# One PSUM tile per prompt head, and an attention end written out for every engine

## The chip, the core and the metric

The kernel runs on one NeuronCore of one Trainium2 chip. The metric is device time in microseconds (us) of one execution. The engines are PE (TensorE matmuls; its weight loads are listed apart as PEld), DVE (VectorE), ACT (ScalarE), POOL (GpSimd) and SP (SyncE, which here only issues loads).

## What is computed

One inference step of a two-layer trunk. Each layer takes 256 prompt tokens and 8 samples of 8 new tokens (320 columns in all) through one input projection, three token mixers, and a gated sum:

```
x += W_out( sum_b sigmoid(gate_b(xn)) * P_b( branch_b(xn) * silu(z_b) ) ), xn = RMSNorm(x)
  A: multi-scale causal pooling mixer
  B: multi-head latent attention (low-rank q and kv, rotary key, absorbed form)
  C: gated DeltaNet
```

Branch B (MLA) has 8 heads. The prompt attends to itself; each sample attends to 2048 cached tokens, gathered by a page table, and to its own 8.

## The kernel before

Values are fp32. A large product is done as three fp32r matmuls per 128 rows of contraction (`mm3`, lines 220 to 222): high weight by high input, high weight by low input, low weight by high input. So each weight block is split first: `split_w` writes the high part `wh` on ACT (line 196) and the low part `wl` on DVE (line 197). An input is split in the same way by `split_x` or `split_y` (`yH` on ACT, line 202; `yL` on DVE, line 203).

Each layer has a projection part, ordered by a scheduler, and then an attention part whose order on PE, DVE, ACT and POOL is the order of the code (`tc.manual_schedule`). The attention part has two stages.

- **Head stage.** The loop `for h in range(11)` goes through the 8 prompt heads as a pipeline. For head h: scores `hsc` on PE (`head_scores`, lines 1278 and 1279), two maxima on DVE (1283, 1284), two exponentials on ACT (1289, 1290, output `pS`). Two steps later come the reciprocal on DVE (1294), the scaling on POOL (1295, 1296), three transposes `pT` on PE (1301) and their copy `pPT` on ACT (1303). One step after that comes `po`, the product with the values (1310), and its use on DVE (1312). Two gate products (`gate`, 24 matmuls each) lie between the heads, one half at a time, and DVE also turns the first sample's keys (`flip`, 1164 and 1167). The scores of all heads are slices of one tile of four PSUM banks. After the heads come the first sample's scores `sc` (1177).
- **Sample stage.** The loop `for bb in range(NB)` goes through the 8 samples. For each one: the exponential, one or two gate products, the transposes `PT` and `PTn`, the 34 matmuls `pv` (1248, 1252), and in the next step the product `olat` (1260), which reorders the result.

Then comes the end of the attention: 24 branch products `br` (3 branches by 8 blocks `m`; 12 matmuls each) with `oml` (32 small matmuls that end the MLA branch) among the first ones, and then the output projection. In `branch(n, m)`, n = 0 is the pooling branch with input y0 = `zs[0:4]`, n = 1 the DeltaNet branch with `zs[8:12]`, and n = 2 the MLA branch with `zs[4:8]`, which is ready only after `oml`. These products stand outside the hand-ordered part, so the scheduler places them; it also puts some of their weight splits back into the sample loop. In layer 1 one gate product is left over after the loop (`if order: gate("A")`), and the scheduler mixes its matmuls with the first branch products. All products rotate through PSUM tiles with tag `A`: four banks during the attention, and after it a newly opened pool (four banks in layer 0, six in layer 1).

Of the kernel before, what the change touches and what calls it, by code (L numbers as in the profile page):

```python
# [116 lines left out]
def trunk(tc, I, O, layers=2):  # L117
# [7 lines left out]
    @contextmanager  # L125
    def phase(name, psum, side="left"):

        with tc.tile_pool(name=name, bufs=1, side=side, reuse_waits="tile") as sb, tc.tile_pool(name=name + "_ps", bufs=1, space=PSUM, reuse_waits="tile") as pp:
            old = dict(banks), dict(wcfg)
            banks.clear()  # L130
            banks.update(pool=pp, n=psum)
            wcfg.clear()
            yield sb
            banks.clear()
            wcfg.clear()
            banks.update(old[0])
            wcfg.update(old[1])

    def ps(tag, name):
        return banks["pool"].tile([128, 512], F32, tag=tag, name=name, bufs=banks["n"][tag])  # L140

# [268 lines left out]
    for l in range(layers):  # L410
# [719 lines left out]
        olat = p2.tile([128, 2, 8, 64], F32, tag="qlat", name="olat", bufs=1)  # L1130
        p2b, pa = enter(f"pa_{l}", dict(A=4, S=1), "right")
        pdc, phc, pbc = ExitStack(), ExitStack(), ExitStack()
        pd = pdc.enter_context(tc.tile_pool(name=f"pd_{l}", bufs=1, reuse_waits="tile"))
# [35 lines left out]
        def scores(keys, q4):  # L1169

            KT, krT = keys
            sc = banks["pool"].tile([128, 4, 512], F32, tag="S", name="sc", bufs=1)
# [143 lines left out]

        def split_y(pool, y0):
            yb[y0] = (pool.tile([128, 4, T], F32R, name=f"yH{y0}"), pool.tile([128, 4, T], F32R, name=f"yL{y0}"))
            for i in range(4):
                split_x(yb[y0][0][:, i, :], yb[y0][1][:, i, :], zs[y0 + i])  # L1320

        def branch(n, m, tag):
            if (n, m) in spilled:
                t = per.tile([128, T], F32, tag="gt", name="gt", bufs=NG)
                nc.gpsimd.dma_start(t, spilled[n, m])
            else:
                if (n, m) not in early:
                    gate("pj")
                t = early[n, m]
            _, wname, y0 = branches[n]  # L1330
            w = split_w(load_w(I[wname][l][:, m * 128 : m * 128 + 128], 4, 128)[:, :4, :], 4)
            b = ps(tag, "br")
            mm3(b[:, :T], w, yb[y0], 4)
            if n == 0:
                accs[m] = p3a.tile([128, T], F32, tag="acc", name="acc", bufs=4)
                stt(accs[m], t, 1.0, b[:, :T], add, mult)
            else:
                stt(t, t, 1.0, b[:, :T], add, mult)
                nc.gpsimd.tensor_tensor(accs[m], accs[m], t, add)


        with tc.manual_schedule(engines={mybir.EngineType.PE, mybir.EngineType.DVE, mybir.EngineType.Activation, mybir.EngineType.Pool}):
# [9 lines left out]
            nm, w = gate_w()  # L1352
            hsc = banks["pool"].tile([128, 4, 512], F32, tag="S", name="hsc", bufs=1)

# [7 lines left out]
            keys = key_tiles()  # L1362
            flips = {3: 0, 4: 1, 5: 2, 6: 3, 7: 4}
            hs, hp = {}, {}
            b = sc = None
            for h in range(11):
                if h < 8:
                    head_scores(h, hsc[:, h % 4])
                    st2 = head_max(hsc[:, h % 4])
                    hs[h] = head_soften(hsc[:, h % 4], st2), st2  # L1370
                if h < 2:
                    values(h)
                if h == 4:
                    gather(1)
                if h in flips:
                    flip(0, keys, flips[h])
# [19 lines left out]
                if h == 9:  # L1396
                    sc = scores(keys, q4)
            phc.close()
            pb = pbc.enter_context(tc.tile_pool(name=f"pb_{l}", bufs=1, side="right", reuse_waits="tile"))
# [38 lines left out]
            wuv = load_wuv(pb.tile([128, 1024], F32, tag="S", name="wuv", bufs=2))  # L1438
            pdc.close()
            p3e = ExitStack()  # L1440
            p3a = p3e.enter_context(tc.tile_pool(name=f"p3a_{l}", bufs=1, reuse_waits="tile"))
            yb = {}
            split_y(p3a, 0)
        branch(0, 0, "A")
        combined(NB - 1, combine(o))
        if order:
            gate("A")
        branch(0, 1, "A")
        b = ps("A", "oml")
        for p in range(4):  # L1450
            for e in range(2):
                h = 2 * p + e
                for cc in range(2):
                    nc.tensor.matmul(b[64 * e : 64 * e + 64, p * 64 : p * 64 + 64], wuv[:, cc, h * 64 : h * 64 + 64], olat[:, cc, h, :], start=cc == 0, stop=cc == 1)
        for p in range(4):
            stt(zs[4 + p][:, TP:], b[:, p * 64 : p * 64 + 64], 0.5, zs[4 + p][:, TP:], mult, mult)
        pbc.close()
        p2b.close()
        p2c.close()
        pec.close()  # L1460


        last = l == layers - 1
        p3c, p3 = enter(f"p3_{l}", dict(pj=2, A=6) if last else dict(pj=4, A=4))
        wcfg.update(pool=p3, n=2)
        split_y(p3, 8)
        split_y(p3, 4)
        mg = (p3.tile([128, 8, T], F32R, name="mgH"), p3.tile([128, 8, T], F32R, name="mgL"))
        xT = p3.tile([128, 8, T], F32, name="xT")
        nc.gpsimd.dma_start(xT, xs[l])  # L1470
        for mp in range(4):
            for n in range(3):
                for m in (2 * mp, 2 * mp + 1):
                    if n or m > 1:
                        branch(n, m, "A")
# [3 lines left out]
        if last:  # L1479

            y6 = [ps("A", "yo") for _ in range(6)]
            t0s = (0, 128, 192)
# [26 lines left out]
        else:  # L1509
# [9 lines left out]
            nc.sync.dma_start(O["y_sample"].rearrange("b s d -> (b s) d"), yo[64:, 2, :])  # L1519
        p3c.close()  # L1520
        p3e.close()
    ctx.close()
# [27 lines left out]
```

## Time and profile before

| | |
|---|---|
| device time, median of 3 runs | 1057.81 us (1056.7 to 1057.89) |
| profiled execution | 1062.18 us |
| its span | 1060.1 us |
| PE busy in the span | 995.1 us (94%) |
| DVE, ACT, POOL busy | 708.6 (67%), 465.0 (44%), 329.5 us (31%) |
| mean granted PE clock | 0.968 of full |

The span is the time from the first to the last instruction in the trace. Times in the trace are in us from the start of the span; layer 0's attention part lies at about 284 to 470 us and layer 1's at about 802 to 990 us.

### The profile page before, as it was taken

Reading aid. Unit: us, or ns where it says so; the run is one execution under the profiler, and the core shown is the slowest. Engines: PE = TensorE matmul, PEld = TensorE weight load, DVE = VectorE, ACT = ScalarE, POOL = GpSimd, SP = SyncE. Lnnn points to the kernel's source line nnn. Section 1 sums busy time; section 2 is a strip of 40 time slices with the busy share of each in tenths; the row PEclk is TensorE's granted clock in tenths of the full one; section 3 lists DMA queues with packets and bytes.
Section 4 is the critical chain, followed back from the end, with each engine's and each line's share of the span. In section 5 each row is a group of like instructions: output and inputs, shape, how many; then the busy total and the mean of one; then the engine's idle time right before and its main releaser. Section 6 shows DMA issues by size and latency. Waiting matters only on the chain. (4 is left out here: it accounts for less than half of the span.)

```text
span 1060.1 us, 24775 instructions
## 1 busy us (share of the span) xinstructions
PE 995.1 (94%) x10211; PEld 869.1 (82%) x10211; DVE 708.6 (67%) x1353; ACT 465.0 (44%) x838; POOL 329.5 (31%) x467
## 2 busy tenths in 40 slices
PE   8989899999989999989989978989999999999996
PEld 6877798887878887779978867979887778777996
DVE  3899984558556666568659878645674657674872
ACT  5554353454543333344546624326445333334453
POOL 3566321215240101035345542212234211000631
PEclk7999999999989999999999979999999999999998
DMA  8533333633746776258563322345264477742861
GB/s 232 154 81 99 100 84 91 182 96 113 211 131 191 245 232 228 79 166 249 141 200 82 99 80 72 99 133 133 81 161 156 150 255 220 248 156 86 262 177 50
DMA packets 202698, 159.22 MB, mean 150 GB/s; under 512 B 27704, under 2 KB 191826, under 8 KB 200010
## 3 DMA queue, kind: packets, MB, share of 16 engines
q1 hardware_dynamic: 176364, 98.47, 34.3%
q0 software_dynamic: 7424, 48.75, 12.8%
q10 hardware_dynamic: 18798, 10.44, 3.4%
q8 instruction: 80, 1.31, 0.5%
q14 instruction: 32, 0.26, 0.1%
HBM read 144.17 MB, written 13.68 MB: 149 GB/s over the span
## 5 line engine op out<-in xcount | busy, mean ns | idle before, releaser
L197 DVE TENSOR_TENSOR wl<-wraw,wh 128x1024 fp32r<-128x1024 f32 (+2 forms) x169 | 195.2, 1164 | 80.3 <-ACT wh L196 79.6
L196 ACT ACTIVATE wh<-wraw 128x1024 fp32r<-128x1024 f32 (+1 forms) x180 | 166.2, 935 | 165.2 <-PE pj L221 77.8
L220 PE MATMUL pj<-xnH,wh 128*128 128x320 f32 (+1 forms) x528 | 175.4, 332 | 16.9 <-DVE V L497 6.1
L222 PE MATMUL pj<-xnH,wl 128*128 128x320 f32 (+1 forms) x528 | 172.4, 327 | 7.4 <-DVE wl L197 7.1
L221 PE MATMUL pj<-xnL,wh 128*128 128x320 f32 (+1 forms) x528 | 170.7, 323 | 0.0
L220 PE MATMUL gate<-xnH,wh 128*128 128x320 f32 x384 | 125.1, 326 | 1.7 <-DVE V L497 1.5
L220 PEld LDWEIGHTS pj<-xnH,wh 128*128 128x128 f32 (+1 forms) x528 | 103.8, 197 | 23.3 <-ACT wh L196 8.3
L222 PE MATMUL gate<-xnH,wl 128*128 128x320 f32 x384 | 120.5, 314 | 1.6 <-DVE wl L197 1.3
L221 PE MATMUL gate<-xnL,wh 128*128 128x320 f32 x384 | 119.7, 312 | 0.0
L222 PEld LDWEIGHTS pj<-xnH,wl 128*128 128x128 f32 (+1 forms) x528 | 103.5, 196 | 11.8 <-DVE wl L197 9.1
L221 PEld LDWEIGHTS pj<-xnL,wh 128*128 128x128 f32 (+1 forms) x528 | 103.7, 196 | 5.2 <-issue 3.8
L220 PEld LDWEIGHTS gate<-xnH,wh 128*128 128x128 f32 x384 | 72.9, 190 | 9.3 <-issue 5.7
L1167 DVE STREAM_TRANSPOSE KT<-kv 128x1024 f32<-128x1024 f32 x64 | 78.6, 1228 | 0.4
L222 PEld LDWEIGHTS gate<-xnH,wl 128*128 128x128 f32 x384 | 72.7, 189 | 3.0 <-DVE wl L197 1.8
L221 PEld LDWEIGHTS gate<-xnL,wh 128*128 128x128 f32 x384 | 73.0, 190 | 1.0 <-issue 0.8
L220 PE MATMUL br<-yH,wh 128*128 128x320 f32 x192 | 59.7, 314 | 5.2 <-ACT wh L196 3.3
L1248 PE MATMUL pv<-kv,PT 128*64 128x256 f32 x512 | 58.8, 382 | 2.3 <-ACT PT L1226 2.3
L1177 PE MATMUL sc<-KT,q 32*64 32x256 f32 x2048 | 59.3, 377 | 0.0
L221 PE MATMUL br<-yL,wh 128*128 128x320 f32 x192 | 59.1, 309 | 0.0
L222 PE MATMUL br<-yH,wl 128*128 128x320 f32 x192 | 58.4, 309 | 0.0
L505 DVE SCALAR_TENSOR_TENSOR cy<-V,prm,cy 128x344 f32<-128x344 f32 x72 | 56.4, 803 | 0.5
L1177 PEld LDWEIGHTS sc<-KT,q 32*64 32x64 f32 x2048 | 45.8, 131 | 12.0 <-issue 5.7
(410 smaller groups left out, 2046.8 us busy)
## 6 DMA issues: line engine op xcount, KB each, us to landing
wraw<-in_w_in SPq DMA_DIRECT2D x114, 512.0 KB
wraw<-in_w_out SPq DMA_DIRECT2D x16, 512.0 KB
q<-q4d SPq DMA_DIRECT2D x64, 72.0 KB
gate<-gt ACTq DMA_DIRECT2D x28, 160.0 KB
gt<-gate POOLq DMA_DIRECT2D x28, 160.0 KB, 3.7
wraw<-in_w_br_pool SPq DMA_DIRECT2D x16, 256.0 KB
wraw<-in_w_br_dn SPq DMA_DIRECT2D x16, 256.0 KB
wraw<-in_w_br_mla SPq DMA_DIRECT2D x16, 256.0 KB
```

The costliest lines, as they stand in the source:

```text
L196: act(h, raw, AF.Copy)
L197: (nc.gpsimd.tensor_tensor if spare or turn[0] in K["lo"] else tt)(lo, raw, h.bitcast(F32), sub)
L220: nc.tensor.matmul(out, wh[:, k, :], xh[:, first + k, :], start=k == 0, stop=False)
L221: nc.tensor.matmul(out, wh[:, k, :], xl[:, first + k, :], start=False, stop=False)
L222: nc.tensor.matmul(out, wl[:, k, :], xh[:, first + k, :], start=False, stop=k == nk - 1)
L505: stt(y, V[:, j : j + 344], wj(j), y, mult, add)
L1167: nc.vector.transpose(v[:, a], kv[:, a * 1024 : a * 1024 + 1024].rearrange("p (i k c) -> p i k c", i=4, k=8))
L1177: nc.tensor.matmul(sc[64 * hf : 64 * hf + 64, g, :256], q4[r, k, :], krT[r, keys_] if k == 8 else KT[r, k, keys_], start=k == 0, stop=k == 8,)
L1248: nc.tensor.matmul(pv[64 * hf : 64 * hf + 64, :256], PT[:, n * 128 + 64 * hf : n * 128 + 64 * hf + 64], kv[:, r : r + 256], start=n == 0, ...
```

## The change

There are four parts.

1. **A PSUM tile per head.** `hsc` becomes a tile of one bank for each head, out of four (tag `H`).
2. **Two moves in the head loop.** The second gate's split (`gate_w`) goes from the end of step 4 to step 5, behind head 5's exponentials. Three flips go one step later.
3. **The end is written out.** `branch` is cut into `branch_w` (load and split of the weight), `branch_mm` (the product) and `branch_out` (its use). Seven branch products, (0,0), (0,1), (1,0), (1,1), (0,2), (2,0) and (2,1), now stand in the hand-ordered part, in a fixed order on all engines. In the last sample's step, y0 is split ahead of the exponential, product (0,0) stands between `PTn` and `pv`, and y8 is split ahead of `pv`. The leftover gate of layer 1 stands behind product (0,1).
4. **Banks kept open.** The four `A` banks get a pool of their own, which stays open to the end of the layer. The pool after the attention has four other banks (layer 0) or two and two (layer 1), so that layer 1's branch products rotate through four banks and no longer six.

```diff
+        apc = ExitStack()
+        banks["A"] = apc.enter_context(tc.tile_pool(name=f"aps_{l}", bufs=1, space=PSUM, reuse_waits="tile"))
...
-            flips = {3: 0, 4: 1, 5: 2, 6: 3, 7: 4}
+            flips = {3: 0, 4: 1, 6: 2, 7: 3, 8: 4}
...
-                    head_scores(h, hsc[:, h % 4])
-                    st2 = head_max(hsc[:, h % 4])
-                    hs[h] = head_soften(hsc[:, h % 4], st2), st2
+                    hsc = hp_.tile([128, 512], F32, tag="H", name="hsc", bufs=4)
+                    head_scores(h, hsc)
+                    st2 = head_max(hsc)
+                    hs[h] = head_soften(hsc, st2), st2
...
+                if h == 5:
+                    nm, w = gate_w()
...
-                if h == 4:
-                    nm, w = gate_w()
...
+                if not more:
+
+                    pdc.close()
+                    p3a = p3e.enter_context(tc.tile_pool(name=f"p3a_{l}", bufs=1, reuse_waits="tile"))
+                    split_hi(p3a, 0)
                 S = soften(bb, sc, mx)
...
+                else:
+                    split_lo(0)
+                    w00 = branch_w(0, 0)
...
+                if not more:
+                    b00 = branch_mm(0, w00, "A")
                 weigh(bb, mx)
+                if not more:
+                    w01 = branch_w(0, 1)
+                    split_y(p3a, 8)
                 o = attend(bb, PT, PTn, mx)
...
+            branch_out(0, 0, b00)
+            b01 = branch_mm(0, w01, "A")
+            if order:
+                gate("A")
+            w10 = branch_w(1, 0)
+            combined(NB - 1, combine(o))
+            b10 = branch_mm(1, w10, "A")
+            branch_out(0, 1, b01)
+            w11 = branch_w(1, 1)
+            b = ps("A", "oml")
...
+            b11 = branch_mm(1, w11, "A")
+            spc.close()
+            pbc.close()
+            mc.close()
+            p2c.close()
+            pec.close()
...
+            p3c, p3 = enter(f"p3_{l}", dict(pj=2, Y=2) if last else dict(pj=4))
+            wcfg.update(pool=p3, n=2)
+            w20 = branch_w(2, 0)
+            split_y(p3, 4)
+            branch_out(1, 0, b10)
+            w02 = branch_w(0, 2)
+            branch_out(1, 1, b11)
+            b02 = branch_mm(0, w02, "A")
+            w21 = branch_w(2, 1)
+            b20 = branch_mm(2, w20, "A")
+            branch_out(0, 2, b02)
+            b21 = branch_mm(2, w21, "A")
+            branch_out(2, 0, b20)
+            branch_out(2, 1, b21)
```

**Heads, on PE.** PE's rows in layer 0 before the change, from `po` of head 1 to the scores of head 5 (a row names line, instruction, output and inputs, and in brackets the engines whose semaphores it waits for):

```order
L1310 MATMUL po<-pPT,vv 64x256 [waits Activation_49]
L1311 MATMUL po<-pPT,vv 64x128
L1278 MATMUL hsc<-kn,qx_2282 128x128 [waits Activation_49]
L1279 MATMUL hsc<-im 128x128
L1278 MATMUL hsc<-kn,qx_2282 128x256
L1279 MATMUL hsc<-im 128x128
L1301 MATMUL pT<-cst,pS 128x128 [waits PE_49,Pool_49]
L1301 MATMUL pT<-cst,pS 128x128 [waits Pool_49]
L1301 MATMUL pT<-cst,pS 128x128
L1310 MATMUL po<-pPT,vv 64x256 [waits Activation_49]
L1311 MATMUL po<-pPT,vv 64x128
L1278 MATMUL hsc<-kn,qx_2283 128x128 [waits Activation_49]
```

The same rows after the change (line numbers are those of the changed file):

```order
L1319 MATMUL po<-pPT,vv 64x256 [waits Activation_49]
L1320 MATMUL po<-pPT,vv 64x128
L1287 MATMUL hsc<-kn,qx_2282 128x128 [waits PE_49]
L1288 MATMUL hsc<-im 128x128
L1287 MATMUL hsc<-kn,qx_2282 128x256
L1288 MATMUL hsc<-im 128x128
L1310 MATMUL pT<-cst,pS 128x128 [waits PE_49,Pool_49]
L1310 MATMUL pT<-cst,pS 128x128 [waits Pool_49]
L1310 MATMUL pT<-cst,pS 128x128
L1319 MATMUL po<-pPT,vv 64x256 [waits Activation_49]
L1320 MATMUL po<-pPT,vv 64x128
L1287 MATMUL hsc<-kn,qx_2283 128x128
```

The order on PE is the same. What moved is the wait: a head's first score matmul waited for ACT, that is for the exponentials of the head before it, and now waits for no exponential of that head.

**The last sample of layer 1, on ACT.** ACT's rows before the change, from the last sample's exponential (`S`). `gt` is a gate's tanh, and `o` the copy of the `pv` result; the `wh` of 128x1024 is the leftover gate's split, the first `gt` ends the gate of the loop, and the second `gt` ends the leftover gate:

```order
L1207 ACTIVATE S,mx<-S,mx 128x1024 [waits DVE_49,Pool_49]
L1208 ACTIVATE so,mx<-so,mx 64x64
L196 ACTIVATE wh<-wraw 128x1024 [waits DMAHW0_49,PE_49,Activation_49]
L461 ACTIVATE gt<-gt 128x320 [waits DVE_49]
L1226 ACTIVATE PT<-PT 128x512 [waits PE_49] x2
L1254 ACTIVATE o<-pv,mx 128x256 [waits DVE_49,PE_49]
L202 ACTIVATE yH_11262<-zs 128x320 x4
L196 ACTIVATE wh<-wraw 128x512 [waits DMAHW7_49,PE_49]
L196 ACTIVATE wh<-wraw 128x512 [waits DMAHW1_49,PE_49,Activation_49]
L461 ACTIVATE gt<-gt 128x320 [waits DVE_49]
L202 ACTIVATE yH_11386<-zs 128x320 x4
L196 ACTIVATE wh<-wraw 128x512 [waits DMAHW0_49,DMASW6_49,DMASW0_49]
```

The same stretch after the change, where y0 (`yH_11207`) is split already and `yH_11304` is y8:

```order
L1216 ACTIVATE S,mx<-S,mx 128x1024 [waits DVE_49,Pool_49]
L1217 ACTIVATE so,mx<-so,mx 64x64
L200 ACTIVATE wh<-wraw 128x512 [waits DMAHW7_49,Activation_49]
L465 ACTIVATE gt<-gt 128x320 [waits DVE_49]
L1235 ACTIVATE PT<-PT 128x512 [waits PE_49,Activation_49]
L1235 ACTIVATE PT<-PT 128x512 [waits PE_49]
L200 ACTIVATE wh<-wraw 128x512 [waits DMAHW0_49,Activation_49]
L1331 ACTIVATE yH_11304<-zs 128x320 x4
L1263 ACTIVATE o<-pv,mx 128x256 [waits DVE_49,PE_49]
L200 ACTIVATE wh<-wraw 128x1024 [waits DMAHW7_49,Activation_49]
L465 ACTIVATE gt<-gt 128x320 [waits DVE_49]
L200 ACTIVATE wh<-wraw 128x512 [waits DMAHW0_49,PE_49,Activation_49]
```

The leftover gate's split went from ahead of `PT` to behind `o`. The gate's tanh (`gt`) and then the split for product (1,0) stand behind it.

**The leftover gate of layer 1, on PE.** PE's rows before the change, in the middle of the leftover gate, whose matmuls alternate with branch product ones:

```order
L222 MATMUL gate<-xnH,wl 128x320
L220 MATMUL gate<-xnH,wh 128x320
L221 MATMUL gate<-xnL,wh 128x320
L221 MATMUL br<-yL_11263,wh 128x320 [waits DVE_49]
L222 MATMUL br<-yH_11262,wl 128x320
L220 MATMUL br<-yH_11262,wh 128x320 [waits Activation_49]
L222 MATMUL gate<-xnH,wl 128x320
L221 MATMUL br<-yL_11263,wh 128x320 [waits DVE_49]
L222 MATMUL br<-yH_11262,wl 128x320
L220 MATMUL br<-yH_11262,wh 128x320 [waits Activation_49]
```

After the change, from the last matmuls of that gate to product (1,0):

```order
L226 MATMUL gate<-xnH,wl 128x320
L224 MATMUL gate<-xnH,wh 128x320
L225 MATMUL gate<-xnL,wh 128x320
L226 MATMUL gate<-xnH,wl 128x320
L1269 MATMUL olat<-cst,o 128x64 x2
L224 MATMUL br<-yH_11304,wh 128x320 [waits Activation_49]
L225 MATMUL br<-yL_11305,wh 128x320
L226 MATMUL br<-yH_11304,wl 128x320 [waits DVE_49]
```

The gate's 24 matmuls now stand in one piece, then `olat`, then product (1,0), whose first matmul waits for ACT and whose third waits for DVE.

## Rows read from the trace of the kernel before

**Rows 1.** The page's first part: busy us (share of span), instructions of each engine.

```profile
PE 995.1 (94%) x10211; PEld 869.1 (82%) x10211; DVE 708.6 (67%) x1353; ACT 465.0 (44%) x838; POOL 329.5 (31%) x467
```

**Rows 2.** Windows by stage: length, PE, PEld, DVE, ACT, POOL, PEclk, DMA, GB/s.

```profile
300.00:306.00 6.00, 3.75 (x23) 2.54 (x21) 4.97 (x10) 3.20 (x10) 3.47 (x4) 1.00 0.72 236
306.00:314.00 8.00, 7.52 (x29) 6.11 (x30) 4.54 (x11) 2.81 (x11) 3.00 (x4) 0.57 0.56 204
458.00:464.00 6.00, 4.08 (x43) 3.75 (x42) 5.94 (x16) 4.99 (x12) 1.61 (x3) 1.00 0.65 204
470.00:480.00 10.00, 10.00 (x69) 10.00 (x70) 9.50 (x17) 4.17 (x8) 8.74 (x11) 1.00 0.80 242
818.00:824.00 6.00, 3.99 (x25) 2.75 (x23) 4.97 (x11) 2.97 (x8) 3.66 (x5) 1.00 0.74 272
824.00:830.00 6.00, 5.29 (x25) 4.02 (x26) 3.82 (x10) 2.33 (x10) 3.00 (x4) 0.72 0.67 239
```

**Rows 3.** Waits, 284 to 326 us; 806 to 862 us answers the same row.

```profile
PE hsc L1278 <- ACT pS L1290: 2.7, 2, 2.0
```

**Rows 4.** PE's timeline, head stages: start, duration, line, out<-in, [idle <-releaser].

```profile
306.48 0.79 PE L1278 MATMUL hsc<-kn,qx 96*128 96x128 f32 x2 [2.05 <-ACT pS L1290]
...
320.02 1.33 PE L1177 MATMUL sc<-KT,q 32*64 32x256 f32 x40
...
824.71 0.49 PE L1278 MATMUL hsc<-kn,qx 96*128 96x128 f32 x2 [2.05 <-ACT pS L1290]
...
836.65 3.71 PE L1177 MATMUL sc<-KT,q 32*64 32x256 f32 x128
```

**Rows 5.** Timelines of ACT and DVE, layer 0's heads.

```profile
302.42 1.07 ACT L196 ACTIVATE wh<-wraw 128x1024 fp32r<-128x1024 f32 x1
...
305.87 0.47 ACT L1290 ACTIVATE pS<-hsc,st 128x256 f32<-128x256 f32 x1
...
303.52 1.22 DVE L197 TENSOR_TENSOR wl<-wraw,wh 128x1024 fp32r<-128x1024 f32 x1 [0.70 <-ACT wh L196]
...
304.77 0.29 DVE L1283 TENSOR_REDUCE st<-hsc 128x1 f32<-128x128 f32 x1
```

**Rows 6.** Waits, 436 to 475 us, then (last row) 956 to 996 us.

```profile
ACT wh L196 <- DMA wraw<-in_w_br_pool: 5.1, 1, 5.1
...
PE br L220 <- ACT wh L196: 2.8, 2, 1.9
...
PE br L220 <- ACT yH L202: 0.9, 1, 0.9
...
PE pv L1248 <- ACT PT L1226: 0.7, 1, 0.7
...
PE br L220 <- ACT wh L196: 0.5, 2, 0.3
```

**Rows 7.** Timelines of ACT, DVE (964.33: layer 1) and PE, ends of attention.

```profile
446.19 0.63 ACT L196 ACTIVATE wh<-wraw 128x512 fp32r<-128x512 f32 x1
...
458.98 1.53 ACT L202 ACTIVATE yH<-zs 128x320 fp32r<-128x320 f32 x4
...
446.38 0.29 DVE L1264 COPY olat<-olat 128x128 f32<-128x128 f32 x1 [2.02 <-PE olat L1260]
...
446.59 0.48 DVE L460 TENSOR_TENSOR gt<-gate,rn 128x320 f32<-128x320 f32 x1
...
446.99 0.68 DVE L197 TENSOR_TENSOR wl<-wraw,wh 128x512 fp32r<-128x512 f32 x1
...
459.47 0.61 DVE L1456 SCALAR_TENSOR_TENSOR zs<-oml,zs 128x64 f32<-128x64 f32 x4
...
460.60 1.69 DVE L203 TENSOR_TENSOR yL<-zs,yH 128x320 fp32r<-128x320 f32 x4
...
964.33 1.23 DVE L197 TENSOR_TENSOR wl<-wraw,wh 128x1024 fp32r<-128x1024 f32 x1 [0.20 <-ACT wh L196]
...
447.16 0.24 PE L1234 MATMUL PTn<-cst,so 64*64 64x64 f32 x1
```

More of the change, by code (lines that the diff above doesn't have):

```diff
@@ L139, in ps @@
     def ps(tag, name):
-        return banks["pool"].tile([128, 512], F32, tag=tag, name=name, bufs=banks["n"][tag])
+        return (banks.get(tag) or banks["pool"]).tile([128, 512], F32, tag=tag, name=name, bufs=banks["n"][tag])
     def enter(*a, **k):
@@ L1130, in trunk @@
         olat = p2.tile([128, 2, 8, 64], F32, tag="qlat", name="olat", bufs=1)
-        p2b, pa = enter(f"pa_{l}", dict(A=4, S=1), "right")
-        pdc, phc, pbc = ExitStack(), ExitStack(), ExitStack()
+        apc = ExitStack()
+        banks["A"] = apc.enter_context(tc.tile_pool(name=f"aps_{l}", bufs=1, space=PSUM, reuse_waits="tile"))
+        banks["n"] = dict(A=4)
+        mc = ExitStack()
+        pa = mc.enter_context(tc.tile_pool(name=f"pa_{l}", bufs=1, side="right", reuse_waits="tile"))
+        pdc, phc, pbc, hpc, spc = (ExitStack() for _ in range(5))
+        bank4 = lambda st, name: st.enter_context(tc.tile_pool(name=f"{name}_{l}", bufs=1, space=PSUM, reuse_waits="tile"))
         pd = pdc.enter_context(tc.tile_pool(name=f"pd_{l}", bufs=1, reuse_waits="tile"))
@@ L1171, in scores @@
             KT, krT = keys
-            sc = banks["pool"].tile([128, 4, 512], F32, tag="S", name="sc", bufs=1)
+            sc = sp.tile([128, 4, 512], F32, tag="S", name="sc", bufs=1)
             for k in range(9):
@@ L1315, in trunk, with split_hi, split_lo, split_y @@
         accs = {}
-        def split_y(pool, y0):
+        yb = {}
+        def split_hi(pool, y0):
             yb[y0] = (pool.tile([128, 4, T], F32R, name=f"yH{y0}"), pool.tile([128, 4, T], F32R, name=f"yL{y0}"))
             for i in range(4):
-                split_x(yb[y0][0][:, i, :], yb[y0][1][:, i, :], zs[y0 + i])
-        def branch(n, m, tag):
+                act(yb[y0][0][:, i, :], zs[y0 + i], AF.Copy)
+        def split_lo(y0):
+            for i in range(4):
+                tt(yb[y0][1][:, i, :], zs[y0 + i], yb[y0][0][:, i, :].bitcast(F32), sub)
+        def split_y(pool, y0):
+            split_hi(pool, y0)
+            split_lo(y0)
+        def branch_w(n, m):
+            wname = branches[n][1]
+            return split_w(load_w(I[wname][l][:, m * 128 : m * 128 + 128], 4, 128)[:, :4, :], 4)
+        def branch_mm(n, w, tag):
+            b = ps(tag, "br")
+            mm3(b[:, :T], w, yb[branches[n][2]], 4)
+            return b
+        def branch_out(n, m, b):
             if (n, m) in spilled:
@@ L1339, in branch @@
                 nc.gpsimd.tensor_tensor(accs[m], accs[m], t, add)
+        def branch(n, m, tag):
+            if (n, m) not in spilled and (n, m) not in early:
+                gate("pj")
+            branch_out(n, m, branch_mm(n, branch_w(n, m), tag))
         with tc.manual_schedule(engines={mybir.EngineType.PE, mybir.EngineType.DVE, mybir.EngineType.Activation, mybir.EngineType.Pool}):
@@ L1352, in trunk @@
             nm, w = gate_w()
-            hsc = banks["pool"].tile([128, 4, 512], F32, tag="S", name="hsc", bufs=1)
+            hp_ = bank4(hpc, "hp")
             def values(t):
@@ L1438, in trunk @@
             wuv = load_wuv(pb.tile([128, 1024], F32, tag="S", name="wuv", bufs=2))
[L1439 to L1454, printed above, removed]
@@ new lines, in trunk @@
+            w10 = branch_w(1, 0)
[4 more added lines that the diff above has]
+            b = ps("A", "oml")
+            for p in range(4):
+                for e in range(2):
+                    h = 2 * p + e
+                    for cc in range(2):
+                        nc.tensor.matmul(b[64 * e : 64 * e + 64, p * 64 : p * 64 + 64], wuv[:, cc, h * 64 : h * 64 + 64], olat[:, cc, h, :], start=cc == 0, stop=cc == 1)
@@ new lines, in trunk @@
+            for p in range(4):
+                stt(zs[4 + p][:, TP:], b[:, p * 64 : p * 64 + 64], 0.5, zs[4 + p][:, TP:], mult, mult)
+            b11 = branch_mm(1, w11, "A")
[4 more added lines that the diff above has]
+            pec.close()
+            last = l == layers - 1
+            p3c, p3 = enter(f"p3_{l}", dict(pj=2, Y=2) if last else dict(pj=4))
+            wcfg.update(pool=p3, n=2)
+            w20 = branch_w(2, 0)
+            split_y(p3, 4)
@@ L1479, in trunk @@
         if last:
-            y6 = [ps("A", "yo") for _ in range(6)]
+            y6 = [ps("A" if i < 4 else "Y", "yo") for i in range(6)]
             t0s = (0, 128, 192)
@@ L1520, in trunk @@
         p3c.close()
+        apc.close()
+        banks.clear()
         p3e.close()
```

27 lines of the change are left out of this document (9 added, 18 removed).

## The prediction

> **What bounds the kernel now.** I read the page's first part, then windows by stage, then the waits and timelines of the two stages that the change touches. PE is busy for 94% of the span, ahead of DVE's 67% [rows 1]. So the change can win only where PE stands idle or runs at a lower clock. The windows show both in the head stages. At 300 to 306 us PE is busy for 3.75 of 6 us, and in the next 8 us the granted clock is 0.57, which means that about 6.9 us ran at 1.2 GHz instead of 2.4. Layer 1 shows the same stage once more: 3.99 of 6 us busy, and then 0.72 over 6 us, about 3.4 us at the low level [rows 2]. At layer 0's end of attention PE is busy for 4.08 of 6 us, and the clock stays full. In the branch products behind it, PE is busy for all of 10 us [rows 2].
>
> The waits name the cause in the heads. PE's score matmuls wait 2.7 us in two places for ACT's exponentials, in each layer [rows 3]. The reader should see the chain in the timelines. The second gate's split takes DVE until 303.52 + 1.22 = 304.74 us, head 5's maximum starts at 304.77, its second exponential at 305.87, and head 6's scores follow only at 306.48, after 2.05 us idle, because all heads share one PSUM tile [rows 4, 5]. In the ends PE waits in layer 0 for weight splits (2.8 us), for the split of y (0.9) and for the copies of PT (0.7), together 4.4 us. In layer 1 the last two have the same size, but the split waits are only 0.5, together 2.1 us [rows 6].
>
> **The change, heads.** The order on PE is unchanged; only the wait for the exponentials goes. It gives 2.7 us per layer [rows 3]. Three waits come in its place. The first is `po` of head 3: it needs the copy pPT, which on ACT now stands behind head 5's exponentials and the moved split of 1.07 us [rows 5]. PE arrives about 1 us early, so I price it at 1.0, the length of that split. The second is head 5's `pT`: its reciprocal stands on DVE behind the split's low half of 1.22 us [rows 5], and POOL's scaling behind the reciprocal. Head 7's scores cover part of it; the bounds are 0 and 1.2, and I take 0.7, since something under a microsecond of matmuls stands between. The third is head 0: its new bank was last read by copies of the projection part, a wait that another product had before; the bounds are 0 and 0.5, and I take 0.2. The net is 2.7 - 1.9 = 0.8 us per layer, 1.6 for both. The flips cost nothing: they move from DVE's stretch before the reciprocals to places where DVE waited anyway, and the first sample's scores, which need them, come after two more gate halves. Without that cover the last flip would cost PE at most its length, which is that of a DVE pass over 1024 columns, about 1.2 us by the split's row [rows 5].
>
> Then the clock. Layer 0 needs 320.02 - 306.48 = 13.54 us from head 6's scores to the sample scores, and layer 1, with the same instructions, 836.65 - 824.71 = 11.94 [rows 4]. The difference, 1.6 us, is the price of the 3.4 us that layer 0 spent more at 1.2 GHz. So there are three such stretches, worth 4.8 us. Both falls came after a stretch whose two waits add up to 2.7 us [rows 3]. After the change that stretch has 1.0 and 0.7; the wait of 1.92 at 458 to 464 us (the longest of [rows 6]) brought no fall. That speaks for fewer falls, but the heads remain a thin stretch of short matmuls, so I cannot say that they vanish. I take an even chance in each layer that a stretch remains and that layer 0's second goes, so that one or two of three remain; the sum uses one, 3.2 us gained, with bounds of 0 and 4.8.
>
> The Trainium skill speaks against this gain ("TensorE: Matmul & The Clock Gate", Part 4: PE-mode transpose): it says that transposes do not count as activity for the clock. The heads' `pT` are transposes, so by that rule the stretch is thinner than PE's busy time shows, all three stretches could stay, and the clock term would be 0 instead of 3.2. No row here separates the two.
>
> **The change, ends.** Before, the scheduler filled PE with whatever was ready. Now the order is fixed, and I walk through it with the durations of [rows 7]. A product of 12 matmuls takes 10.00 / 69 x 12 = 1.74 us [rows 2].
>
> - *PTn*, both layers: it takes the bank that the gate's product leaves, which DVE empties after the new split for product (0,0). That split's high half ends at 446.19 + 0.63 = 446.82; the low half, the olat copy and the gate's pass add 0.68 + 0.29 + 0.48, so PTn starts at about 448.2, not 447.16 [rows 7]: 1.0 us. DVE's y0 splits before it (1.69) end at about 446.1, and the high halves lie in ACT's idle time ahead of the exponential; they cost nothing here, and up to 1.5 if the exponential had to wait for them.
> - *Product (0,0)* ahead of `pv` hides the PT copies: they end about 1.5 us after PTn, the product about 1.8 after. So the waits of 0.7 and 0.9 go in both layers.
> - *Product (0,2)*, both layers: its split stands behind y4's, which waits for `oml`. From the end of `oml`, DVE's row is: wait for the high half of (2,0) 0.63, its low half 0.68, y4 1.69, a gate product's use 0.48, and the low half of (0,2) 0.68, together 4.16 [rows 7]; the use of `oml` (0.61) and ACT's y4 (1.53) run beside. PE has product (1,1), 1.74, and the first two matmuls, 0.3. The rest is 2.1; instructions overlap slightly, so 2.0.
> - *The leftover gate*, layer 1 only: its split, which lay ahead of PT, now stands behind the copy of `pv`'s result (about 0.47). High half 1.07 [rows 5] and low half 1.23 [rows 7] give 2.8 us after `pv`; product (0,1) and two matmuls cover 2.0: 0.8 us.
> - *Product (1,0)*, layer 1 only: its split now stands behind the gate's own end on DVE and ACT, 0.48 and about 0.5, then 0.63 and 0.68, together 2.3; `olat` and two matmuls cover 0.7: 1.6 us.
>
> Layer 0 gains 4.4 - 1.0 - 2.0 = 1.4; layer 1 loses 1.0 + 0.8 + 1.6 + 2.0 - 2.1 = 3.3. The ends together lose 1.9 (bounds: +1 if the two waits at (0,2) overlap better, -4 if PTn and (0,2) cost half as much again). The banks kept open cost nothing: layer 0's products ran through four banks before, and PE had no idle time there [rows 2].
>
> **The sum.** 1.6 + 3.2 - 1.9 = 2.9 us faster. The profiled execution took 1062.18 us, 2.1 over its span of 1060.1, and lies 4.4 above the median of 1057.81; a difference carries over, so 1057.8 - 2.9 = 1054.9. A measurement of this kernel tells about 0.2%, or 2.1 us, from no change.
>
> **The rivals.**
> - *The clock stays as it was*, all three stretches. For it: the thin stretch of short matmuls remains; the skill's rule above belongs here. Against it: the 2.05 us wait is gone. Then 1.6 - 1.9 = -0.3: 1058.1, no change.
> - *No low clock in either head stage.* For it: the new waits are shorter than the 1.92 that brought no fall. Then the gain is 1.6 + 4.8 - 1.9 = 4.5: 1053.3.
> - *Loads decide the ends, and it is slower.* ACT waited 5.1 us for a pooling weight in layer 0 [rows 6], and other products ran meanwhile. In the fixed order product (0,2) needs such a weight, and nothing may pass it. If the load comes as late against its split as before, 5.1 - 2.0 = 3.1 us more are idle per layer: 2.9 - 6.2 = -3.3, so 1061.1. It turns to a loss when the load is over 1.5 us later than the split's turn in both layers. Against it: that load now starts when the split of (0,1) frees its buffer, ahead of `pv`'s end, some microseconds earlier.
>
> **How the numbers follow.** I give the forecast 0.42 (its own range 1053 to 1057), no low clock 0.22, the clock unchanged 0.18, late loads 0.18. Most of the first two is beyond 0.2%, the third is within it with some on the slow side, the last slower: faster 0.57, same 0.23, slower 0.20. The range of 1051 to 1059.5 reaches below the second case by the bound of the ends, and leaves out most of the last.
>
> **What would show it.** Right: no wait of PE's scores for the exponentials; waits of about 1.0 and 0.7 us at `po` and `pT` in heads 3 to 5; the granted clock over the heads higher in at least one layer; in the ends, waits of PE at (0,2) in both layers and at (1,0) and the gate in layer 1, for ACT's and DVE's splits. Wrong: a clock of 0.57 and 0.72 again; PE waiting for a split that itself waits for DMA; or layer 1's end without the waits at the gate and at (1,0), in which case the gain is larger.

## The result, and the profile after

The changed kernel took 1044.66 us (median of 4 runs, 1039.42 to 1046.31), against 1057.58 for the kernel before beside it: a ratio of 0.9864, 95% interval 0.9835 to 0.9893. It is 12.9 us faster. The forecast was 1054.9 us, in a range of 1051 to 1059.5. So the direction was right, and the size was not: 2.9 us were forecast.

The page's first part answers to [rows 1]. PE has 7.5 us less busy time for the same 10211 matmuls, and the span is 17.3 us shorter (1042.8 against 1060.1; the profiled execution of before, 1062.18, lay 4.6 us over its median, that of after, 1044.80, at its median).

```profile
PE 987.6 (95%) x10211; PEld 865.2 (83%) x10211; DVE 712.1 (68%) x1353; ACT 466.5 (45%) x838; POOL 332.2 (32%) x467
```

To find the place, I cut both traces at the same instructions: layer by layer at the first `kn` (the product ahead of the head stage), the first `sc`, the last `sc`, and the first output projection product. The windows of the kernel before, with the columns of [rows 2]; the first number behind the bounds is the length:

```profile
0.00:283.06 283.06, 264.50 (x2559) 233.53 (x2559) 203.87 (x396) 135.42 (x221) 108.14 (x157) 0.95 0.47 125
283.06:320.02 36.96, 34.21 (x172) 25.90 (x172) 17.44 (x40) 15.89 (x52) 15.88 (x21) 0.91 0.51 172
320.02:441.86 121.84, 120.87 (x1793) 98.79 (x1793) 79.80 (x148) 42.57 (x79) 13.52 (x25) 1.00 0.62 202
441.86:501.36 59.50, 55.01 (x412) 51.44 (x396) 41.46 (x84) 26.72 (x52) 24.30 (x31) 1.00 0.65 197
501.36:800.26 298.90, 275.84 (x2683) 249.41 (x2681) 208.66 (x392) 140.19 (x223) 106.24 (x150) 0.96 0.43 116
800.26:836.65 36.39, 32.81 (x172) 24.35 (x173) 17.44 (x40) 15.89 (x52) 15.89 (x21) 0.95 0.50 174
836.65:958.92 122.27, 121.08 (x1793) 98.91 (x1793) 79.80 (x148) 42.57 (x79) 13.54 (x25) 1.00 0.64 203
958.92:1019.11 60.19, 58.06 (x435) 54.71 (x420) 45.07 (x86) 28.81 (x54) 22.79 (x30) 1.00 0.67 199
```

The same cuts in the changed kernel:

```profile
0.00:281.40 281.40, 263.00 (x2558) 232.31 (x2559) 203.58 (x396) 136.06 (x221) 108.18 (x157) 0.96 0.47 126
281.40:313.81 32.41, 31.01 (x172) 23.63 (x173) 17.24 (x40) 15.89 (x52) 15.88 (x21) 1.00 0.58 197
313.81:435.33 121.52, 120.87 (x1793) 98.78 (x1793) 79.20 (x147) 42.16 (x78) 13.52 (x25) 1.00 0.61 200
435.33:493.81 58.48, 56.09 (x411) 52.70 (x396) 44.78 (x85) 26.92 (x52) 24.39 (x31) 0.97 0.70 206
493.81:783.20 289.39, 271.89 (x2683) 247.12 (x2681) 208.51 (x392) 141.10 (x223) 106.99 (x150) 0.96 0.44 120
783.20:815.68 32.48, 30.76 (x173) 23.73 (x173) 17.23 (x40) 15.90 (x52) 15.89 (x21) 1.00 0.55 194
815.68:937.28 121.60, 120.99 (x1794) 98.84 (x1793) 79.20 (x147) 42.16 (x78) 13.55 (x25) 1.00 0.62 202
937.28:1001.79 64.51, 60.27 (x435) 56.05 (x420) 47.48 (x88) 29.47 (x55) 24.65 (x31) 0.97 0.64 190
```

The reader should go down the two lists line by line: the projection part of layer 0, its head stage, its samples, its end, and then the same for layer 1 (whose first line holds also layer 0's output projection).

| stage | before | after | difference |
|---|---|---|---|
| layer 0: projection | 283.06 | 281.40 | -1.7 |
| heads | 36.96 | 32.41 | -4.6 |
| samples | 121.84 | 121.52 | -0.3 |
| end | 59.50 | 58.48 | -1.0 |
| layer 1: projection | 298.90 | 289.39 | -9.5 |
| heads | 36.39 | 32.48 | -3.9 |
| samples | 122.27 | 121.60 | -0.7 |
| end | 60.19 | 64.51 | +4.3 |

Both heads gained, more than forecast, and the granted clock there is 1.00 (2.4 GHz throughout) instead of 0.91 and 0.95. Layer 0's end gained and layer 1's end lost, as forecast. The largest single difference is in layer 1's projection part, which the diff does not touch and on which the prediction has no word.

**The waits of the heads** answer to [rows 3]; the third row is layer 1's. PE's scores wait for no exponential any more. PE waits instead where it was forecast, at head 3's `po` (forecast 1.0) and head 5's `pT` (forecast 0.7, the same row in both layers). The third forecast wait, at head 0 (0.2), does not show in either layer:

```profile
PE po L1319 <- ACT pPT L1312: 0.8, 1, 0.8
...
PE pT L1310 <- POOL pS L1305: 0.6, 1, 0.6
...
PE po L1319 <- ACT pPT L1312: 1.1, 1, 1.1
```

**The waits of the ends** answer to [rows 6]. The first three rows are layer 0's waits, the others PE's timeline in layer 1. In layer 0 the waits at product (0,2) are 0.7 for the high half and 0.8 for the low half (forecast 2.0 together), and PTn waits 0.7 (forecast 1.0). In layer 1 the gate waits 0.53 (forecast 0.8), product (1,0) 1.21 (forecast 1.6), and product (0,2) 0.69 + 0.81:

```profile
PE br L226 <- DVE wl L201: 0.8, 1, 0.8
...
PE br L224 <- ACT wh L200: 0.7, 1, 0.7
...
PE PTn L1243 <- DVE olat L1273: 0.7, 1, 0.7
...
952.64 0.41 PE L226 MATMUL gate<-xnH,wl 128*128 128x320 f32 x1 [0.53 <-DVE wl L201]
...
957.74 0.41 PE L224 MATMUL br<-yH,wh 128*128 128x320 f32 x1 [1.21 <-ACT wh L200]
...
965.42 0.41 PE L224 MATMUL br<-yH,wh 128*128 128x320 f32 x1 [0.69 <-ACT wh L200]
...
966.78 0.41 PE L226 MATMUL br<-yH,wl 128*128 128x320 f32 x1 [0.81 <-DVE wl L201]
```

**Layer 1's projection part** holds a stretch that begins with the delta net's last 52 `KK` matmuls and ends ahead of the next gate's first matmul. Before the change, its window and PE's longest waits in it:

```profile
685.05:738.54 53.49, 49.34 (x652) 44.80 (x651) 26.50 (x46) 25.84 (x41) 10.96 (x16) 1.00 0.48 130
...
PE pj L220 <- ACT cout L835: 1.4, 1, 1.4
...
PE ktv L846 <- ACT ktv L864: 0.8, 1, 0.8
...
PE pj L220 <- ACT wh L196: 0.8, 1, 0.8
...
PE pj L222 <- DVE wl L197: 0.7, 1, 0.7
```

After the change:

```profile
672.44:721.07 48.63, 47.89 (x652) 44.61 (x652) 26.59 (x46) 25.83 (x41) 10.77 (x16) 1.00 0.51 143
...
PE W L864 <- DVE ke L856: 0.5, 1, 0.5
...
PE pj L224 <- ACT cout L839: 0.3, 1, 0.3
```

The same 652 matmuls take 4.9 us less: PE's idle time falls from 4.15 to 0.74 us (length less busy time), and its busy time by 1.45. Before, PE waited 1.4 us for a copy of the delta net (`cout`), 0.8 for another, and 0.8 and 0.7 for the two halves of a weight split. After, 0.5 (which was there before, too) and 0.3 us are left. PE's order in this stretch differs between the kernels: the scheduler puts the projection products `pj` at other places among the delta net's small matmuls. ACT's and DVE's orders differ here, too: two weight splits come 15 and 22 us into the stretch instead of 26 and 32. Which engine's order makes the difference is not separated. In the rest of this part, and in all of layer 0's projection part, PE's order is the same. The clock is 1.00 in both stretches.

### The profile page after: what moved, and what is told of

Read it like the earlier page. It is cut to its first block, busy times and chain, and to the rows that moved or that the text cites. A ratio compares the mean times of both kernels' runs of the same rounds, so it can differ in the third digit from the quotient of the medians.

```text
span 1042.8 us, 24809 instructions
## 1 busy us (share of the span) xinstructions
PE 987.6 (95%) x10211; PEld 865.2 (83%) x10211; DVE 712.1 (68%) x1353; ACT 466.5 (45%) x838; POOL 332.2 (32%) x467
## 4 chain that ended last, share of the span: by engine, by line
PE 73%; DVE 16%; ACT 5%; issue 3%; DMA 2%; POOL 1%; SPq 0%; DVEq 0%; ACTq 0%; POOLq 0%
PE sc L1186 6%; PE pv L1257 6%; PE pj L224 5%; PE gate L224 5%; PE pj L226 5%; PE pj L225 5%; PE gate L226 5%; PE gate L225 4%; DVE cy L509 4%; DVE wl L201 3%; PE br L226 3%; PE br L224 3%; PE br L225 3%; PE wo L224 2%; PE wo L225 2%
## 5 line engine op out<-in xcount | busy, mean ns | idle before, releaser
L224 PE MATMUL pj<-xnH,wh 128*128 128x320 f32 (+1 forms) x528 | 172.7, 327 | 13.0 <-DVE V L501 7.6
L226 PE MATMUL pj<-xnH,wl 128*128 128x320 f32 (+1 forms) x528 | 170.2, 322 | 6.3 <-DVE wl L201 6.0
L225 PE MATMUL pj<-xnL,wh 128*128 128x320 f32 (+1 forms) x528 | 168.6, 319 | 0.0
```

What stands on the lines that cost most here:

```text
L224: nc.tensor.matmul(out, wh[:, k, :], xh[:, first + k, :], start=k == 0, stop=False)
L225: nc.tensor.matmul(out, wh[:, k, :], xl[:, first + k, :], start=False, stop=False)
L226: nc.tensor.matmul(out, wl[:, k, :], xh[:, first + k, :], start=False, stop=k == nk - 1)
```

## The experiments

In the windows below, a stage is cut as above, and the stretch just shown is called the *KK stretch*. "Order A" is PE's order in layer 1's projection part in the kernel before (ACT's and DVE's go with it), "order B" that of the changed kernel. The kernel before itself spread from 1051.75 to 1063.36 us in the 25 runs beside the first four experiments (median 1058.98), and from 1051.89 to 1061.85 in the 13 beside the next four, so total times say little below some 4 us, and the stages say more. Each stage row is from one profiled execution.

**1. Only the tile per head** (order A).

```diff
-                    head_scores(h, hsc[:, h % 4])
-                    st2 = head_max(hsc[:, h % 4])
+                    hsc = hp_.tile([128, 512], F32, tag="H", name="hsc", bufs=4)
+                    head_scores(h, hsc)
+                    st2 = head_max(hsc)
```

> The kernel before with only a PSUM tile per head; the split, the flips and the ends stay as before, and PE's order in layer 1's projection part too. Theory (the heads' wait and the clock behind it are worth 7 to 8 us over both layers): 1050 to 1052 us, no low clock between 284 and 330 us and in layer 1's heads. Rival (the clock falls there whatever the tiles): only the waits go, 1.6 us, 1056. PE's idle time of some 4 us in layer 1's projection part stays under both.

Measured: 1053.65 us, ratio 0.9955 (0.9926 to 0.9984), which lies between the two theories. The heads of layer 0, of layer 1, and the KK stretch:

```profile
281.84:314.40 32.56, 30.74 (x172) 23.61 (x172) 17.37 (x40) 15.91 (x52) 15.93 (x21) 1.00 0.57 196
...
795.86:829.79 33.93, 32.11 (x176) 25.19 (x172) 17.39 (x40) 15.91 (x52) 15.93 (x21) 0.95 0.53 185
...
678.04:733.78 55.74, 52.29 (x651) 47.84 (x651) 26.51 (x46) 25.84 (x41) 10.96 (x16) 0.94 0.46 125
```

The heads gain 4.4 and 2.5 us. Layer 0 keeps the full clock, layer 1 does not (0.95), and that costs 33.93 - 32.56 = 1.4 us. So the theory is right for layer 0 and not for layer 1. The KK stretch is at its old length and worse: its clock is 0.94. By the ratios the heads alone are worth about a third of the change (0.9955 against 0.9864).

**2. Only the ends and the open banks** (one tile for the heads, old steps; order B).

```diff
+            hall = hp_.tile([128, 4, 512], F32, tag="H", name="hsc", bufs=1)
...
-                    hsc = hp_.tile([128, 512], F32, tag="H", name="hsc", bufs=4)
+                    hsc = hall[:, h % 4]
```

> The changed kernel with one four-bank tile for all heads again and the split and flips at their old steps, so the ends, the open banks and the changed PE order in layer 1's projection part alone. Theory (that order is worth about 5 us, the ends lose 3): 1055 to 1057 us with the low clock in the heads back. Rival (the projection part's gain is only the clock's chance): about 1061.

Measured: 1051.20 us, ratio 0.9954 (0.9923 to 0.9985), faster than both theories. Layer 0's heads and end, layer 1's heads, the KK stretch, and PE's wait in layer 1's heads:

```profile
281.13:317.63 36.50, 32.88 (x172) 24.42 (x172) 17.46 (x40) 15.91 (x52) 15.93 (x21) 0.95 0.50 175
...
439.16:496.11 56.95, 54.55 (x412) 51.18 (x397) 44.86 (x85) 27.21 (x53) 24.20 (x31) 1.00 0.71 209
...
785.86:820.29 34.43, 31.04 (x172) 23.53 (x172) 17.46 (x40) 15.92 (x52) 15.93 (x21) 1.00 0.53 184
...
674.84:723.72 48.88, 47.88 (x651) 44.61 (x651) 26.60 (x46) 25.84 (x41) 10.78 (x16) 1.00 0.51 142
...
PE hsc L1287 <- ACT pS L1299: 3.4, 3, 2.1
```

The last window settles the main point: with the old heads, order B has its 48.88 us. The low clock came back in layer 0's heads (0.95) and not in layer 1's. The third row shows the old heads at full clock: 34.43 us, with 3.4 us of waits for exponentials in three places (the last row). Against it, the new heads (32.48) gain 1.95 us without any help of the clock: their waits are 1.7 us instead of 3.4, and PE's busy time is 0.3 less.

What the clock cost the kernel before follows from the same row. In layer 0 it is 36.96 - 34.43 = 2.5 us. Layer 1's old stage has one more wait, which the 34.43 do not hold: head 0's scores wait for the copies of `kn`. The windows of [rows 3] begin behind it, at 806 us:

```profile
805.10 0.49 PE L1278 MATMUL hsc<-kn,qx 96*128 96x128 f32 x2 [0.86 <-ACT kn L1125]
```

So the clock cost 36.39 - 0.86 - 34.43 = 1.1 us in layer 1. Layer 0 of this experiment has the same wait of 0.86 and one fall of the clock, and gives nearly the same price: 36.50 - 0.86 - 34.43 = 1.2. The wait for `kn` shows in three of the six head stages profiled with one tile for all heads, and in none of the 16 with a tile per head. Why it comes in one layer and not in the other is not traced.

**3. Layer 1's end left to the scheduler** (order B).

```diff
+WRITTEN = (0,)
...
+            if l in WRITTEN:
+                branch_out(0, 0, b00)
```

> The changed kernel with layer 1's end left to the scheduler as before (layer 0's stays written out). Theory (the written order of layer 1's end costs 4.3 us by waits for splits): 1040 to 1041 us. Rival (the time from the last pv to the output projection only looks longer because work moved into it): 1044 to 1045.

Measured: 1043.95 us, ratio 0.9891 (0.9833 to 0.9948), so the total lies nearer the rival, and with runs from 1042.92 to 1048.52 it does not separate the theories. In the profiled run layer 1's projection part is 3.7 us longer than in the changed kernel (293.05 us from cut to cut) with the same order on PE, which hides what the end gains. Layer 0's end, layer 1's end:

```profile
434.83:491.78 56.95, 54.56 (x412) 51.17 (x396) 45.16 (x86) 27.96 (x53) 24.21 (x31) 1.00 0.71 211
...
939.27:1000.14 60.87, 58.05 (x435) 54.70 (x420) 44.66 (x87) 28.94 (x54) 24.37 (x31) 1.00 0.65 197
```

Layer 1's end takes 60.87 instead of 64.51: the written order costs 3.6 us there, and 2.7 against the repeat at full clock (63.59, experiment 5). Layer 0's written end takes 56.95 when the clock stays full, here and in experiment 2, 2.5 us less than before.

**4. Layer 0's end left to the scheduler**, old steps in the heads (order A).

```diff
+WRITTEN = (1,)
```

> The changed kernel with layer 0's end left to the scheduler, and the split and flips at their old steps; PE's order in layer 1's projection part is then the one of before. Theory (that order costs about 5 us, layer 0's end 1, the old steps 0 to 2): 1050 to 1053 us, with PE's 4 us idle in that part back. Rival (the order is worth nothing): 1045 to 1047.

Measured: 1057.86 us, ratio 0.9988 (0.996 to 1.0016), slower than either theory: no gain is left that stands out from the spread. Heads of layer 0, of layer 1, and the KK stretch:

```profile
282.76:316.90 34.14, 32.32 (x172) 25.13 (x172) 17.37 (x40) 15.91 (x52) 15.92 (x21) 0.95 0.54 185
...
799.08:833.01 33.93, 32.11 (x176) 25.19 (x173) 17.39 (x40) 15.92 (x52) 15.93 (x21) 0.95 0.54 185
...
681.33:736.98 55.65, 52.25 (x651) 47.79 (x651) 26.50 (x46) 25.84 (x41) 10.92 (x16) 0.94 0.46 125
```

Order A is back and with it the long stretch, 55.65 us, 7.0 more than order B, with a clock of 0.94. Its waits for `cout` and for the two halves of the split are those of the kernel before (1.4, 0.8 and 0.7 us). Both heads fell to 0.95. Layer 1's written end takes 64.48 us from cut to cut (954.78 to 1019.26), at clock 0.97, and takes back most of what the heads still gain. Experiments 2 to 4 together place the cause: order B is there when layer 0's end is written out, whatever the heads and layer 1's end are, with the banks kept open in all three.

**5. The changed kernel again**, beside the next three.

> The changed kernel once more, beside the next ones on one chip. Theory: 1043 to 1047 us, heads 32.4 us in each layer with no low clock, layer 1's end 63 to 64.5. Rival (the first result was a good chance of the clock): 1050 or more, with low clock in the heads.

Measured: 1044.24 us, ratio 0.9897 (0.9834 to 0.9961). Its head stages take 32.43 and 32.49 us at clock 1.00, its layer 1 end 63.59 at 1.00. The result holds.

**6. The moves in the head loop undone** (order B).

```diff
-            flips = {3: 0, 4: 1, 6: 2, 7: 3, 8: 4}
+            flips = {3: 0, 4: 1, 5: 2, 6: 3, 7: 4}
...
-                if h == 5:
-                    nm, w = gate_w()
...
+                if h == 4:
+                    nm, w = gate_w()
```

> The changed kernel with the second gate's split and the flips at their old steps; PE's order in layer 1's projection part is that of the changed kernel. Theory (the moves shorten no wait but thicken PE's work where the clock fell): a low-clock stretch of 3.4 us in at least one head stage, 1.4 us each, so 0 to 3 us above the changed kernel. Rival (the moves are what removes the waits): heads 2 us longer in each layer, 4 us above.

Measured: 1045.22 us, ratio 0.9888 (0.9835 to 0.9941), 1.0 us above the changed kernel beside it, as the theory has it and within the spread. The heads, and PE's one wait in layer 0's:

```profile
282.43:314.99 32.56, 30.75 (x173) 23.61 (x173) 17.36 (x40) 15.89 (x52) 15.89 (x21) 1.00 0.57 198
...
783.70:817.51 33.81, 32.01 (x172) 24.70 (x172) 17.35 (x40) 15.88 (x52) 15.89 (x21) 0.95 0.54 186
...
PE po L1319 <- ACT pPT L1312: 1.8, 1, 1.8
```

At full clock the old steps cost 0.1 us (32.56 against 32.43). But layer 1's clock fell again. Over all profiles, the new tiles with the old steps show a lowered clock in 4 of 6 head stages, and with the moves in none of 10. The moves save almost no wait: they put two waits, 0.8 to 1.1 and 0.6 us, in the place of one of 1.8. That the clock stays for this reason is likely, and not shown by itself.

**7. The leftover gate's split early** (order B).

```diff
                     w01 = branch_w(0, 1)
+                    lg = gate_w() if order else None
                     split_y(p3a, 8)
...
-            if order:
-                gate("A")
+            if lg:
+                lb = gate_mm("A", lg[1])
             w10 = branch_w(1, 0)
+            if lg:
+                gate_out(lg[0], lb)
```

> The changed kernel with two things moved in layer 1's end: the leftover gate's split ahead of the y8 split, and the split for product (1,0) ahead of the gate's use. Theory (waits for splits cost layer 1's end 3 to 4 us): the waits at the gate (0.5) and at (1,0) (1.4) go, and the low clock behind them, so layer 1's end takes 60.5 to 62 us, 2 to 3.5 less than in the changed kernel. Rival (the time sits in the product (0,2) and the order of the branches): 64 us as in the changed kernel.

Measured: 1043.31 us, ratio 0.9858 (0.9806 to 0.9911). Layer 1's end:

```profile
943.47:1003.93 60.46, 58.07 (x436) 54.69 (x420) 45.89 (x86) 28.24 (x54) 22.30 (x30) 1.00 0.68 199
```

60.46 us, 3.1 less than the same end in the run beside it (63.59), and about what it took before (60.19). PE has no wait at the gate and at (1,0) any more, and still 0.73 and 0.81 at (0,2): so those two places are what layer 1's written order lost. The total does not tell this run from the changed kernel.

**8. The kernel before with filler on PE in the heads** (a third PE order in layer 1's projection part).

```diff
+                    if h in (4, 5, 6, 7):
+                        f = ps("A", "fill")
+                        for _ in range(4):
+                            nc.tensor.matmul(f[:, :T], xn[0][:, 0, :128], xn[0][:, 0, :], start=True, stop=True)
                     head_scores(h, hsc[:, h % 4])
```

> The kernel before with 16 products of 320 columns put ahead of the scores of heads 4 to 7 (their result is not used), 0.6 us in each place; the waits for the exponentials stay. Theory (a low clock in the heads costs 1.5 to 2.5 us besides the waits): no low clock in the head stages, heads 34 to 35.5 us although PE does 2.4 us more work there, against 37.0 and 36.4 before. Rival (the waits alone make the time): heads 37 us or more.

Measured: 1054.35 us, ratio 0.998 (0.9956 to 1.0004). The heads:

```profile
281.02:316.14 35.12, 33.83 (x188) 25.90 (x188) 17.45 (x40) 15.92 (x52) 15.93 (x21) 1.00 0.52 182
...
794.39:830.57 36.18, 34.05 (x193) 25.82 (x189) 17.48 (x40) 15.92 (x52) 15.94 (x21) 1.00 0.50 174
```

The clock is 1.00 in both stages, as expected. Layer 0's heads are 1.8 us shorter than before with more work on PE; layer 1's only 0.2 shorter, outside the expected range. Layer 1 has the wait of 0.86 for `kn` again, and layer 0 has not; without it the two stages take 35.1 and 35.3 us. The filler also covers part of the waits: one of 1.3 us for an exponential is left of 2.7. So the theory is half borne out: with the stretch filled, the clock stays, which is worth 2.5 us in layer 0 and only 1.1 in layer 1, and against the old heads at full clock (34.43) the filler costs 0.7 and 0.9.

**9. Gate's split early, and product (0,2) ahead of y4's split** (nearly order B).

```diff
+            w02 = branch_w(0, 2)
             w20 = branch_w(2, 0)
-            split_y(p3, 4)
             branch_out(1, 0, b10)
-            w02 = branch_w(0, 2)
-            branch_out(1, 1, b11)
             b02 = branch_mm(0, w02, "A")
+            split_y(p3, 4)
+            branch_out(1, 1, b11)
```

> The changed kernel with the leftover gate's split and the split for (1,0) moved as in the run before it, and in both layers the split for product (0,2) and that product ahead of y4's split. Theory (the waits at (0,2), 1.5 us per layer, come from the splits that stand ahead of it): layer 0's end 55 to 57 us instead of 58.5, without the low clock; layer 1's end 59 to 60.5; in all 2 to 6 us below the changed kernel, which is about 1040 to 1043 us. Rival (product (2,0) then waits for y4 as long as (0,2) did before): ends as in the run with the gate's split alone, 1043 to 1045 us.

Measured: 1039.67 us, ratio 0.9825 (0.9796 to 0.9854), the fastest here; the interval still overlaps that of the changed kernel. The profile is that of its slowest run (1049.88). Layer 0's end, layer 1's end, in it PE's one long wait and ACT's wait behind it, and the KK stretch:

```profile
440.26:495.13 54.87, 54.02 (x411) 51.17 (x396) 42.56 (x86) 28.00 (x53) 24.82 (x31) 1.00 0.73 219
...
945.53:1006.86 61.33, 57.80 (x436) 54.68 (x420) 44.17 (x87) 28.96 (x55) 24.46 (x31) 1.00 0.66 198
...
975.37 0.41 PE L224 MATMUL br<-yH,wh 128*128 128x320 f32 x1 [2.69 <-ACT wh L200]
...
974.69 0.63 ACT L200 ACTIVATE wh<-wraw 128x512 fp32r<-128x512 f32 x1 [4.62 <-DMA wraw<-in_w_br_pool]
...
678.11:729.29 51.18, 49.38 (x651) 45.97 (x651) 26.60 (x46) 25.71 (x41) 10.66 (x16) 0.97 0.49 136
```

Layer 0's end takes 54.87 us, 3.6 less, without a low clock. Layer 1's end takes 61.33 instead of the expected 59 to 60.5: PE waits 2.69 us for a split that itself waits 4.62 us for a pooling weight's load. This is the mechanism of the third rival, though at the next pooling product, (0,3), which the scheduler places, and not at (0,2). ACT waits for such loads in other runs, too, and splits and products ahead of them hide most of it from PE: in the changed kernel's repeat ACT waits 4.22 us for that load and PE 0.22 us for the split. The KK stretch, whose order inside is B, takes 51.18 us in this profile, where its clock fell.

## Why the prediction was wrong

**The step that failed** is the list itself: the working takes "the two stages that the change touches", prices heads and ends, and puts everything else at nothing without a reason, as if the order outside the attention part stood still. It does not. The scheduler gives layer 1's projection part another order when layer 0's end is written out. Six profiles with order B have a KK stretch of 48.5 to 48.9 us; the kernel before has 53.49 with order A, and experiments 1 and 4, also with order A, have 55.74 and 55.65, where the clock fell as well. That is 4.9 us, and up to 7.0 with the clock, that the sum lacks. With these 4.9 the forecast would have been 1050.0, already outside the range. (Experiment 9's 51.18, at clock 0.97, shows that order B is no guarantee.) Both orders could be read before the run. What in the scheduler's rules makes the difference was not looked into.

**Heads, waits.** The mechanism was right: no wait for exponentials, and new waits of 0.8 to 1.1 and 0.6 us at the two named places. The net was mis-sized: 1.6 us were forecast for both layers, and the runs show 4.8. Of these, 3.9 are twice 34.43 - 32.48 (measured in layer 1, and taken for layer 0 as well): at full clock PE's scores wait 3.4 us for exponentials, in three waits, not the 2.7 read from a stage that ran partly at low clock, and the new waits are 1.7, not 1.9. The other 0.9 is layer 1's wait for `kn`, which the working did not see. It expected a new wait of 0.2 at that place instead.

**Heads, clock.** Forecast 3.2 us, measured 2.5 + 1.1 = 3.6. That the two are near is luck: the forecast took two of three low stretches away at 1.6 us each, and all three went, worth 1.2 each. My chance for that case was 0.22; the even chance per layer was too low, for I counted only the waits and gave the moves no credit. The 4 of 6 lowered stages without the moves against none of 10 with them (experiment 6) speak for the moves.

**The Trainium skill's rule** ("TensorE: Matmul & The Clock Gate", Part 4: PE-mode transpose), that transposes do not count as activity, would have left the clock low as I applied it. The trace does not agree with that use: with the moves, all ten head stages kept 1.00 with their transposes unchanged. That does not refute the rule, but the consequence that I drew from it fell. The Trainium skill's page "Perfetto Trace Analysis" (Optimization Strategy) says that the same gap repeated on the engine that should be busy can mean too little SBUF or PSUM for the next tile. The trace agrees: a bank per head took 4.4 us out of layer 0's heads, waits and clock together.

**Ends.** Forecast: layer 0 gains 1.4, layer 1 loses 3.3. Measured: layer 0 gains 1.0 in the profiled run and 2.5 where its clock stays full; layer 1 loses 4.3, of which about 1 (64.51 - 63.59) goes with the low clock (0.97) that the repeat did not show. The waits stand at the places of the walk, each somewhat smaller than forecast. So layer 1's loss of 3.4 us at full clock (63.59 - 60.19) agrees with the forecast of 3.3 partly by luck: PE's waits there grew only from 2.1 to 4.5 us, and the rest is not traced. What the walk left out is that the clock can fall behind its waits: the changed kernel has a low stretch in layer 0's end in both its profiles, while experiments 2 and 3 kept the full clock there with the same waits.

**The sum.** Of the 17.3 us between the two profiles, 8.5 are the heads, 4.9 the KK stretch and 1.0 the samples; the ends take back 3.3. The other 6 or so lie in projection stretches with the same PE order in both, where the lowered clock falls on other matmuls from run to run. The profiled run of before lay 4.6 over its median, which takes up most of that; some 2 us stay in the spread of the runs. Against the forecast of 2.9 us, the sum lacks 4.9 for the KK stretch, 3.2 for the heads' waits, 0.4 for their clock and 1.0 for the samples, and has 1.4 too much for the ends: put right, it gives 11.0 of the 12.9 measured. Why the samples gained was not traced. The working's 0.2% for what a measurement can tell was too small as well: the kernel before spread over 11.6 us in 25 runs.

**The rivals.** The clock as it was: false. No low clock in the heads: true, and its 1053.3 us are still 8.6 too slow, for it lacks the same terms. Late loads: not at (0,2) in the changed kernel, where PE's waits are 0.7 and 0.8 us for the split itself; at (0,3) in experiment 9.

## What to carry to other kernels

Where a scheduler orders part of a program, compare its order in every part, not only in the part that the diff names: 4.9 us, more than the whole forecast gain, sat in a stretch that nobody edited. A written order for all engines wins where a wait is long and known, and loses where a split lands behind an unrelated wait; walking the in-order queues with measured durations found the places of both here. A wait read at a lowered clock is not the wait at full clock (2.7 and 3.4 us for the same heads), so a price needs a stage at one clock. And a wait on PE can cost more than its length when the clock falls behind it: 0.9 and 1.5 us more in the two ends.

## What the runs showed of the hardware

In the head stages the clock fell to its 1.2 GHz level after stretches in which no single idle time of PE was over 2.05 us [rows 4], and in the changed kernel's ends after waits of at most 1.21 us. One such fall cost 1.1 to 1.6 us in a head stage of 34 to 37 us, and the twice as long one in layer 0 of the kernel before 2.5 us. The waits alone did not decide whether it came: the old heads ran at 0.95 in one layer and at 1.00 in the other (experiment 2), and so did the new tiles with the old steps (experiments 1 and 6); layer 1's end of the changed kernel ran at 0.97 in one execution and at 1.00 in another. And the spread of one and the same kernel was wide: 1051.75 to 1063.36 us for the kernel before, 1036.37 to 1049.88 for the fastest.
